# A four-layer fp32 trunk on one core: the two halves of each split weight side by side, and weight buffers at another spacing

## The chip, the core and the metric

The kernel runs on one core of one Trainium2 chip. The metric is the device time of one execution in microseconds (us). The kernel before took 2257.87 us, the median of three runs (2257.78 to 2258.11).

A core has five engines that run side by side and meet only through semaphores: TensorE (in the profile PE, and PEld for its weight loads), VectorE (DVE), ScalarE (ACT), GpSimd (POOL) and SyncE (SP), which here issues the transfers. A matmul on PE holds one operand still in its array (the weights, loaded by an instruction of its own, LDWEIGHTS) and streams the other, the moving operand, past it. Both are read from the on-chip memory SBUF, which has 128 partitions; a "word" below is one fp32 number in each partition.

## What is computed

One sequence of 256 tokens of width 2048 goes through two layers in fp32, each a mixer and a gated feed-forward part, and a last RMSNorm. What matters here is the many products of activations with large weight matrices; attention, scans and norms are small beside them.

```python
h = x
for layer in range(2):
    hn = rms_norm(h, mix_norm_w[layer])
    mix = even_mixer(hn, ...) if layer % 2 == 0 else odd_mixer(hn, od_w_in[0], od_w_out[0])
    h = h + mix
    hn = rms_norm(h, ffn_norm_w[layer])
    g = causal_dwconv(hn @ w_gate[layer], conv_w[layer], conv_b[layer])   # 2048 -> 5632
    h = h + (silu(g) * (hn @ w_up[layer])) @ w_down[layer]                # 5632 -> 2048
return rms_norm(h, final_norm_w)
```

## The kernel before, in words

**Split operands.** Every large product is made from two fp32r parts of each operand: `hi`, the value rounded to fp32r by a copy, and `lo`, what the rounding left over. Three of the four cross products are summed: hi by hi, hi by lo, and lo by hi. An activation tile (`x`, `o` or `act` in the profile) is 128x512: 256 tokens of hi, then 256 tokens of lo.

**A panel.** Weights come from memory in panels of four row blocks (`CH` = 4) of 128 rows and 256 columns, 512 KB each. `prep` (L111) makes one panel ready: SP issues its transfer into a `raw` tile (L122), ACT writes hi with a cast (L127, `hl<-raw`), and DVE writes lo as raw minus hi (L128, `hl<-raw,hl`). Both halves go into one tile `hl`, in the order (c t n): block c, half t (0 is hi, 1 is lo), column n. So 256 words of hi stand ahead of 256 words of lo, and every run that is read or written is 256 words long. The pool `wraw` has four buffers and `whl` three; an `hl` buffer is 4*544 + 8 = 2184 words, so its three buffers start 2184 words apart.

**Three ways to use a panel.** `chan` (L143) takes the weights as the operand that stays in the array: each 128 columns of one half of `hl` are loaded (LDWEIGHTS), and an activation tile streams past. A hi half (L149) meets all 512 words of the activation tile, hi and lo at once; a lo half (L158) meets the 256 hi words alone. A panel has 4 blocks x 2 column halves, so 8 matmuls of 512 and 8 of 256. Their order: six hi matmuls (three blocks of each column half), four lo, one hi, four lo, one hi. `tok` (L161) is the other way round: activations stay, and `hl` streams, for the attention values (L168, L175) and the first panel group (L180). `wide` (L355) does the same with panels of 2 blocks by 512 columns in the last product of the kernel (L361), where the second half of a panel's six matmuls per token tile uses lo.

**Who uses which.** `products` (L184) walks over a stage's jobs and panels: it calls `prep`, then the job's kind, then lets one step of the background work (attention, scan, norms) be emitted by `tick`. The gate and up products of both feed-forward parts, q and k of both mixers, the convolution and gate inputs of the even one, both output projections and the first down projection (`project`, L321) are `chan`; `finish` (L366) calls `prep` itself and uses `wide`.

**What sets the order.** The engines run their instructions in program order. A cast waits for its transfer and for its `hl` buffer to be free, that is for the last matmul of the panel three before it. A hi matmul waits for the cast (ACT), a lo matmul for the subtraction (DVE).

Of the kernel before, what the change touches and what calls it, by code (L numbers as in the profile page):

```python
# [10 lines left out]
F32R = mybir.dt.float32r  # L11
# [4 lines left out]
P = 128  # L16
# [6 lines left out]
CH = 4  # L23
# [38 lines left out]
class Trunk:  # L62
# [45 lines left out]
        return self.params[:, o : o + n]  # L108


    def prep(self, src, pieces=1, between=None):  # L111

        nc = self.nc
        ch, ncol = src.shape[-2:]
        raw = self.wraw.tile([P, CH * 272], F32, tag="raw", name=self.nm("raw"))[:, : ch * ncol]
        hl = self.whl.tile([P, CH * 544 + 8], F32R, tag="hl", name=self.nm("hl"))[:, : 2 * ch * ncol]
        raw = raw.rearrange("p (c n) -> p c n", n=ncol)
        hl = hl.rearrange("p (c t n) -> p c t n", t=2, n=ncol)
        n = ch // pieces
        parts = [slice(i * n, (i + 1) * n) for i in range(pieces)]  # L120
        for i, s in enumerate(parts):
            nc.sync.dma_start(raw[:, s], src[:, s])  # L122
            if between is not None:
                between(i)
        for s in parts:
            hi, lo = hl[:, s, 0, :], hl[:, s, 1, :]
            nc.scalar.copy(hi, raw[:, s])  # L127
            nc.vector.tensor_tensor(lo, raw[:, s], hi.bitcast(F32), ALU.subtract)  # L128
        return hl
# [55 lines left out]
    def products(self, jobs, xs, order=None, late=False):  # L185

        state = [None] * len(jobs)
        waiting = []  # L190

        def chunk(i, ci):
            kind, panel, done = jobs[i]
            od = order or range(panel.shape[0])
            if ci == 0:
                state[i] = self.banks(self.aux if late and i == 2 else self.acc)
            if late and i == ci == 0:
                hl = self.prep(panel[od[ci]], CH, xs.load)
            else:
                hl = self.prep(panel[od[ci]])  # L200
            kind(state[i], hl, xs, od[ci] * CH, ci == 0, ci == len(od) - 1)
            if waiting and i == 2 and ci:
                waiting.pop(0)()
            if ci == len(od) - 1:
                if late and i < 2:
                    waiting.append(lambda: done(state[i]))
                else:
                    done(state[i])
            self.tick()

        n = [j[1].shape[0] for j in jobs]
        for ci in range(n[0]):
            chunk(0, ci)
            chunk(1, ci)
        for i in range(2, len(jobs)):
            for ci in range(n[i]):
                chunk(i, ci)
# [774 lines left out]
```

## Time and profile before

| | |
|---|---|
| time, median of 3 | 2257.87 us |
| profiled execution, its own time | 2258.26 us |
| its span, first to last instruction | 2256.5 us |
| mean granted TensorE clock | 0.999 |
| weights and other data read from memory | 410.86 MB, 183 GB/s over the span |
| transfer of one 512 KB panel, issue to landing | 3.5 us (median) |
| mean busy share of the transfer engines | 55.5% for the queue of the panels |

How to read it: a row of a group names line, engine, operation, out<-in tiles and shapes, then the count; behind the bar stand the busy time in us, the mean of one in ns, and the idle time of the engine just ahead of the group, with what ended it. Matmuls overlap, so the mean of one (some 390 ns for a 512-wide one) is its way through the array and not what it adds; what it adds is the distance from its start to the next start. In the timeline, neighbours of one kind are merged: start, length, engine, line, and how many (x4).

### The profile page before, as it was taken

How to read it: one execution, taken by the hardware profiler on the slowest of the kernel's cores; microseconds unless marked ns; L12 is line 12 of the kernel's file. 1: busy time of each engine (PE TensorE's matmuls, PEld its weight loads, DVE VectorE, ACT ScalarE, POOL GpSimd, SP SyncE). 2: the span in 40 equal slices, each digit the busy share in tenths (PEclk: the TensorE clock that was granted, in tenths of full speed). 3: DMA queues.
4: the chain of work that ended last, by engine and by line, in shares of the span. 5: the costliest groups of instructions: out<-in, count | busy, mean ns of one | idle time of the engine just before them, and what ended most of it. 6: DMA issues, size and time to landing. Idle time of an engine off the chain costs nothing.

```text
span 2256.5 us, 32580 instructions
## 1 busy us (share of the span) xinstructions
PE 2240.3 (99%) x12554; PEld 1941.8 (86%) x12554; DVE 1451.5 (64%) x2025; ACT 1140.9 (51%) x1690; POOL 197.1 (9%) x202
## 2 busy tenths in 40 slices
PE   8999999999999999999999999999999999999998
PEld 7888888888888888888888888888888888888886
DVE  7767767666666665555566656676666666654444
ACT  7555554555555554444444444546555555553343
POOL 3014111101010100000000000110010101000000
PEclk9999999999999999999999999999999999999999
DMA  6654455555555555555555555565555555555554
GB/s 230 189 178 142 152 180 187 186 188 188 190 190 188 187 187 189 189 190 188 187 176 170 172 166 177 177 204 185 180 188 187 189 191 188 187 188 192 189 190 155
DMA packets 116251, 415.08 MB, mean 184 GB/s; under 512 B 12912, under 2 KB 15488, under 8 KB 115968
## 3 DMA queue, kind: packets, MB, share of 16 engines
q1 hardware_dynamic: 115776, 412.48, 55.5%
q8 instruction: 98, 1.61, 0.3%
q14 instruction: 57, 0.47, 0.1%
q10 hardware_dynamic: 288, 0.52, 0.1%
q0 software_dynamic: 32, 0.01, 0.0%
HBM read 410.86 MB, written 2.10 MB: 183 GB/s over the span
## 4 chain that ended last, share of the span: by engine, by line
PE 98%; DVE 0%; ACT 0%; DMA 0%; issue 0%; SPq 0%; POOL 0%; DVEq 0%
PE acc L149 52%; PE acc L158 27%; PE acc L361 11%; PE acc L168 4%; PE acc L175 2%; PE aux L556 0%; PE aux L587 0%; DMA raw<-in_wev 0%; PE acc L180 0%; PE aux L578 0%; PE aux L817 0%; PE aux L539 0%; PE aux L797 0%; PE aux L555 0%; PE aux L588 0%
## 5 line engine op out<-in xcount | busy, mean ns | idle before, releaser
L128 DVE TENSOR_TENSOR hl<-raw,hl 128x1024 fp32r<-128x1024 f32 (+1 forms) x779 | 958.1, 1231 | 712.4 <-ACT hl L127 711.9
L127 ACT CAST hl<-raw 128x1024 fp32r<-128x1024 f32 (+1 forms) x779 | 814.3, 1046 | 872.4 <-PE acc L149 600.4
L149 PE MATMUL acc<-x,hl 128*128 128x512 f32 x3904 | 1078.3, 395 | 0.0
L149 PEld LDWEIGHTS acc<-x,hl 128*128 128x128 f32 x3904 | 700.5, 188 | 106.7 <-issue 0.7
L158 PEld LDWEIGHTS acc<-x,hl 128*128 128x128 f32 x3904 | 596.5, 188 | 64.7
L158 PE MATMUL acc<-x,hl 128*128 128x256 f32 x3904 | 618.3, 280 | 0.0
L361 PE MATMUL acc<-hl,act 128*128 128x512 f32 x1056 | 243.4, 392 | 0.0
L361 PEld LDWEIGHTS acc<-hl,act 128*128 128x128 f32 x1056 | 198.2, 188 | 45.1
L149 PE MATMUL acc<-act,hl 128*128 128x512 f32 x704 | 192.2, 394 | 0.0
L229 ACT COPY ev<-acc 128x256 f32<-128x256 f32 x244 | 90.9, 373 | 162.1 <-PE acc L149 162.1
L457 POOL TENSOR_TENSOR cv<-cv,rbc 128x256 f32<-128x256 f32 x88 | 93.5, 1081 | 880.0 <-ACT cv L456 880.0
L149 PEld LDWEIGHTS acc<-act,hl 128*128 128x128 f32 x704 | 126.3, 188 | 19.4
L149 PE MATMUL acc<-o,hl 128*128 128x512 f32 x512 | 140.9, 395 | 0.0
L299 POOL TENSOR_TENSOR sum<-sum,sq 128x256 f32<-128x256 f32 x67 | 62.3, 929 | 731.9 <-ACT sq L298 723.6
L158 PEld LDWEIGHTS acc<-act,hl 128*128 128x128 f32 x704 | 107.5, 188 | 11.7
L230 DVE TENSOR_TENSOR ev<-acc,ev 128x256 f32<-128x256 f32 x244 | 102.5, 421 | 22.2 <-ACT ev L229 18.3
L158 PE MATMUL acc<-act,hl 128*128 128x256 f32 x704 | 111.4, 280 | 0.0
L149 PEld LDWEIGHTS acc<-o,hl 128*128 128x128 f32 x512 | 92.0, 188 | 14.2
L168 PE MATMUL acc<-hl,x 128*128 128x512 f32 x352 | 103.3, 401 | 0.0
L158 PEld LDWEIGHTS acc<-o,hl 128*128 128x128 f32 x512 | 78.3, 188 | 8.6
L158 PE MATMUL acc<-o,hl 128*128 128x256 f32 x512 | 81.1, 280 | 0.0
L168 PEld LDWEIGHTS acc<-hl,x 128*128 128x128 f32 x352 | 61.1, 188 | 7.9 <-DVE k L618 0.3
(173 smaller groups left out, 1081.0 us busy)
## 6 DMA issues: line engine op xcount, KB each, us to landing
raw<-in_wg SPq DMA_DIRECT2D x176, 512.0 KB, 3.5
raw<-in_wu SPq DMA_DIRECT2D x176, 512.0 KB, 3.5
raw<-in_wd SPq DMA_DIRECT2D x176, 512.0 KB, 3.5
raw<-in_wod SPq DMA_DIRECT2D x96, 512.0 KB, 3.5
raw<-in_wev SPq DMA_DIRECT2D x84, 512.0 KB, 3.5
raw<-in_wevo SPq DMA_DIRECT2D x32, 512.0 KB, 4.0
raw<-in_wodo SPq DMA_DIRECT2D x32, 512.0 KB, 3.5
h<-in_x SPq DMA_DIRECT2D x16, 128.0 KB, 4.8
```

The costliest lines, as they stand in the source:

```text
L127: nc.scalar.copy(hi, raw[:, s])
L128: nc.vector.tensor_tensor(lo, raw[:, s], hi.bitcast(F32), ALU.subtract)
L149: mm(accs[nt], hl[:, k, 0, nt * P : (nt + 1) * P], xs[k0 + k], start=start and k == 0, stop=stop and k == CH - 1,)
L158: mm(accs[nt][:, :T], hl[:, k, 1, nt * P : (nt + 1) * P], xs[k0 + k][:, :T], start=False, stop=False)
L168: both = lambda k: mm(accs[tt], part(xs[k0 + k], 0, tt), hl[:, k].rearrange("p t n -> p (t n)"), start=start and k == 0, stop=stop and k = ...
L175: mm(accs[tt][:, :T], part(xs[k0 + k], 1, tt), hl[:, k, 0, :], start=False, stop=False)
L229: nc.scalar.copy(t, acc[:, T:])
L230: nc.vector.tensor_tensor(t, acc[:, :T], t, ALU.add)
L299: nc.gpsimd.tensor_tensor(sums[-1], sums[-1], sq, ALU.add)
L361: self.nc.tensor.matmul(acc, part(xs[k0 + k], p), hl[:, k, w, :], start=start and n == k == 0, stop=stop and n == 2 and k == ch - 1,)
L457: nc.gpsimd.tensor_tensor(c, c, self.rbc, ALU.mult)
```

## The change

`prep` gets an argument `pairs`. With it, `hl` is laid out in the order (c n t): for each block and column, hi and lo are neighbours. Hi is then every second word from word 0, lo every second from word 1. The cast writes every second word; the subtraction reads hi at every second word and writes lo at every second; a weight load of `chan` reads 128 words out of a stretch of 256. `products` asks for it wherever the job's kind is `chan`, apart from the very first panel, which is a `tok` one. Panels of `tok` and `wide` keep the old order.

Every `hl` tile, of all three kinds, is also made 8 words longer (2192 words) and used from word 16 on, so its buffers start 2192 words apart rather than 2184, and everything placed behind them moves by a little.

```diff
-    def prep(self, src, pieces=1, between=None):
+    def prep(self, src, pieces=1, between=None, pairs=False):
...
-        hl = self.whl.tile([P, CH * 544 + 8], F32R, tag="hl", name=self.nm("hl"))[:, : 2 * ch * ncol]
+        hl = self.whl.tile([P, CH * 544 + 16], F32R, tag="hl", name=self.nm("hl"))[:, 16 : 16 + 2 * ch * ncol]
         raw = raw.rearrange("p (c n) -> p c n", n=ncol)
-        hl = hl.rearrange("p (c t n) -> p c t n", t=2, n=ncol)
+        if pairs:
+            hl = hl.rearrange("p (c n t) -> p c t n", t=2, n=ncol)
+        else:
+            hl = hl.rearrange("p (c t n) -> p c t n", t=2, n=ncol)
...
-                hl = self.prep(panel[od[ci]])
+                hl = self.prep(panel[od[ci]], pairs=kind == self.chan)
```

No instruction is added, taken away or moved on any engine. On DVE and ACT one thing shows in the rows of the program: a panel's split is one run in the new order where it had four. DVE near its start before, in program order (operation, out<-in tiles, shape; the first row is a panel of `chan`, the last but one a panel of `tok`):

```order
L128 TENSOR_TENSOR hl_181<-raw_180,hl_181 128x4x256 [waits DMAHW0_49,Activation_49]
L306 SCALAR_TENSOR_TENSOR x_202<-h_83,first,x_202 128x256 [waits DMAHW1_49,Activation_49]
L306 SCALAR_TENSOR_TENSOR x_206<-h_83,first,x_206 128x256 [waits DMAHW2_49,Activation_49]
L306 SCALAR_TENSOR_TENSOR x_210<-h_83,first,x_210 128x256 [waits DMAHW3_49,Activation_49]
L306 SCALAR_TENSOR_TENSOR x_214<-h_83,first,x_214 128x256 [waits DMAHW4_49,Activation_49]
L128 TENSOR_TENSOR hl_229<-raw_228,hl_229 128x4x272 [waits DMAHW5_49,Activation_49]
L128 TENSOR_TENSOR hl_258<-raw_257,hl_258 128x4x256 [waits DMAHW6_49,Activation_49]
```

The same place of the changed kernel (its lines are numbered 4 higher):

```order
L132 TENSOR_TENSOR hl_181<-raw_180,hl_181 128x1024 [waits DMAHW0_49,Activation_49]
L310 SCALAR_TENSOR_TENSOR x_202<-h_83,first,x_202 128x256 [waits DMAHW1_49,Activation_49]
L310 SCALAR_TENSOR_TENSOR x_206<-h_83,first,x_206 128x256 [waits DMAHW2_49,Activation_49]
L310 SCALAR_TENSOR_TENSOR x_210<-h_83,first,x_210 128x256 [waits DMAHW3_49,Activation_49]
L310 SCALAR_TENSOR_TENSOR x_214<-h_83,first,x_214 128x256 [waits DMAHW4_49,Activation_49]
L132 TENSOR_TENSOR hl_229<-raw_228,hl_229 128x4x272 [waits DMAHW5_49,Activation_49]
L132 TENSOR_TENSOR hl_258<-raw_257,hl_258 128x1024 [waits DMAHW6_49,Activation_49]
```

Only the shape differs, on 640 rows of DVE and on 640 casts of ACT; order and waits are the same.

On PE the one difference is in `wide`, at the kernel's end. The first six matmuls of the first panel there, before (hl_18420 streams; act_14032 and act_14039 are the weights):

```order
L361 MATMUL acc_18417<-hl_18420,act_14032 128x512 [waits Activation_49]
L361 MATMUL acc_18417<-hl_18420,act_14039 128x512 [waits DVE_49]
L361 MATMUL acc_18417<-hl_18420,act_14032 128x512
L361 MATMUL acc_18417<-hl_18420,act_14039 128x512
L361 MATMUL acc_18417<-hl_18420,act_14032 128x512
L361 MATMUL acc_18417<-hl_18420,act_14039 128x512
```

And of the changed kernel:

```order
L365 MATMUL acc_18417<-hl_18420,act_14032 128x512 [waits Activation_49]
L365 MATMUL acc_18417<-hl_18420,act_14039 128x512
L365 MATMUL acc_18417<-hl_18420,act_14032 128x512
L365 MATMUL acc_18417<-hl_18420,act_14039 128x512
L365 MATMUL acc_18417<-hl_18420,act_14032 128x512 [waits DVE_49]
L365 MATMUL acc_18417<-hl_18420,act_14039 128x512
```

The wait for DVE's subtraction stands three matmuls later, at the first one that uses lo; this is so in each of the 88 panels of `wide`.

## The prediction

> **What bounds the kernel now.** The page's busy shares come first, then the clock row, then the chain that ended last with its shares by line.
>
> ```profile
> span 2256.5 us, 32580 instructions
> PE 2240.3 (99%) x12554; PEld 1941.8 (86%) x12554; DVE 1451.5 (64%) x2025; ACT 1140.9 (51%) x1690; POOL 197.1 (9%) x202
> PEclk9999999999999999999999999999999999999999
> by line: PE acc L149 52.4%; PE acc L158 26.6%; PE acc L361 10.8%; PE acc L168 3.6%; PE acc L175 1.8%; PE aux L556 0.3%; PE aux L587 0.3%; DMA raw<-in_wev 0.2%; PE acc L180 0.2%; PE aux L578 0.2%; issue 0.2%; PE aux L817 0.2%; PE aux L539 0.
> ```
>
> PE is busy throughout at full clock, and the chain is PE alone. A busy PE need not be PE at its peak, so I look for waits inside it: the matmul groups of `chan`.
>
> ```profile
> L149 PE MATMUL acc<-x,hl 128*128 128x512 f32 x3904 | 1078.3, 395 | 0.0
> L158 PE MATMUL acc<-x,hl 128*128 128x256 f32 x3904 | 618.3, 280 | 0.0
> L149 PE MATMUL acc<-act,hl 128*128 128x512 f32 x704 | 192.2, 394 | 0.0
> L158 PE MATMUL acc<-act,hl 128*128 128x256 f32 x704 | 111.4, 280 | 0.0
> L149 PE MATMUL acc<-o,hl 128*128 128x512 f32 x512 | 140.9, 395 | 0.0
> L158 PE MATMUL acc<-o,hl 128*128 128x256 f32 x512 | 81.1, 280 | 0.0
> ```
>
> No idle time stands ahead of any of them. There are 3904 + 704 + 512 = 5120 hi matmuls and as many lo ones; 8 of each make a panel, so 640 panels change their order of words. By the chain a hi matmul takes 52.4% of 2256.5 us / 5120 = 230.9 ns, a lo one 26.6% of it / 5120 = 117.2 ns. The kernel is a row of such slots, and only what lengthens or shortens a slot, or starves PE, can move the time. The timeline shows the slots, with the weight loads below them.
>
> ```profile
> 1001.71 1.79 PE L149 MATMUL acc<-act,hl 128*128 128x512 f32 x7
> 1003.33 0.64 PE L158 MATMUL acc<-act,hl 128*128 128x256 f32 x4
> 1003.81 0.39 PE L149 MATMUL acc<-act,hl 128*128 128x512 f32 x1
> 1004.04 0.64 PE L158 MATMUL acc<-act,hl 128*128 128x256 f32 x4
> 1004.52 1.79 PE L149 MATMUL acc<-act,hl 128*128 128x512 f32 x7
> ...
> 1008.95 0.62 PE L158 MATMUL acc<-act,hl 128*128 128x256 f32 x4
> 1009.40 0.39 PE L149 MATMUL acc<-act,hl 128*128 128x512 f32 x1
> ```
>
> ```profile
> 1003.10 0.66 PEld L158 LDWEIGHTS acc<-act,hl 128*128 128x128 f32 x4
> 1003.70 0.19 PEld L149 LDWEIGHTS acc<-act,hl 128*128 128x128 f32 x1
> 1003.82 0.19 PEld L158 LDWEIGHTS acc<-act,hl 128*128 128x128 f32 x1
> ```
>
> A panel lasts 1004.52 - 1001.71 = 2.81 us. A load starts as the matmul before its own starts (1003.82 against 1003.81), so it is hidden by one slot and no more. How long the load occupies its path comes from two widths.
>
> ```profile
> L149 PEld LDWEIGHTS acc<-x,hl 128*128 128x128 f32 x3904 | 700.5, 188 | 106.7 <-issue 0.7 <-ACT ev L229 0.2 <-ACT v L631 0.2
> L817 PEld LDWEIGHTS aux<-ex,ssd 128*64 128x64 f32 x32 | 1.6, 134 | 2.0 <-issue 2.0
> ```
>
> 64 columns more cost 188 - 134 = 54 ns, so 128 columns take some 108 ns of reading. **In a lo slot that leaves 117.2 - 108 = 9 ns; in a hi slot 123 ns.** This margin carries the prediction: a slower load is paid 5120 times in lo slots, and hidden in hi slots until it takes over twice as long.
>
> **The change part by part.** (1) Strided weight loads, 10,240 of them. No row shows a load with a stride, so I bound it. If each word costs what it costs now, 108 ns still fit: nothing. If two words came with one access and now only one is used, the load takes 216 ns: hi slots still hide it (230.9), lo slots grow by 216 - 117.2 = 98.8 ns, times 5120 = +506 us. Between these, the nearest row is the moving operand of the same slot: L158 streams 256 adjacent words in 117.2 ns. A strided load crosses the same 256 words. The moving path thus covers at least that stretch in one lo slot; a load path of like width would need up to 117.2 ns, and with the 9 ns that now follow a load, up to 126 ns: +9 x 5120 = +46 us. I take nothing, since the moving path proves that 256 adjacent words per slot can be delivered, and keep +46 us as an end.
>
> [...]
>
> (2) The cast and the subtraction with a stride.
>
> ```profile
> L128 DVE TENSOR_TENSOR hl<-raw,hl 128x1024 fp32r<-128x1024 f32 x772 | 951.8, 1233 | 707.9 <-ACT hl L127 707.7
> L127 ACT CAST hl<-raw 128x1024 fp32r<-128x1024 f32 x772 | 809.6, 1049 | 871.5 <-PE acc L149 600.4 <-PE acc L361 139.6 <-ACT cv L456 36.9
> ```
>
> ```profile
> 1004.99 1.05 ACT L127 CAST hl<-raw 128x1024 fp32r<-128x1024 f32 x1 [1.76 <-PE acc L149]
> 1006.08 1.23 DVE L128 TENSOR_TENSOR hl<-raw,hl 128x1024 fp32r<-128x1024 f32 x1 [1.52 <-ACT hl L127]
> ```
>
> No row has a stride here either: the ends are nothing and double. The cast starts when PE gives up the buffer (1004.99) and the subtraction ends at 1007.31. The three buffers give the panel to PE two panels later, at about 1004.99 + 2 x 2.81 = 1010.6, so the chain of the two has 3.3 us to spare; doubled (+1.05 + 1.23 = 2.28 us) it still arrives. What can run out is DVE's total. Its load by stage:
>
> ```profile
> 30.00:430.00 400.00, 399.09 (x2319) 345.81 (x2318) 295.13 (x461) 218.57 (x340) 64.18 (x61) 1.00 0.53 173
> 430.00:560.00 130.00, 130.00 (x747) 113.66 (x746) 87.73 (x128) 68.89 (x104) 13.22 (x12) 1.00 0.57 189
> 560.00:1000.00 440.00, 440.00 (x2517) 384.35 (x2516) 278.31 (x380) 220.73 (x314) 35.26 (x33) 1.00 0.57 188
> 1500.00:1650.00 150.00, 150.00 (x873) 131.29 (x872) 101.24 (x157) 82.67 (x127) 13.25 (x18) 1.00 0.57 190
> 1650.00:2000.00 350.00, 350.00 (x2003) 305.72 (x2003) 235.56 (x344) 188.20 (x283) 34.76 (x32) 1.00 0.57 188
> ```
>
> (The third pair is DVE, the fourth ACT.) In the first stage DVE has 400 - 295.13 = 104.9 us free for some 130 such panels (400 / 2.81 = 142, less a dozen of `tok`), 0.8 us each: L128 may go from 1.23 to 2.0 us unseen. Doubled, it overruns by 295 + 160 - 400 = 55 us there; with 46, 157, 53 and 125 panels (length / 2.81) in the other four the overruns are 14, 31, 17 and 39 us: +156 us in all. ACT doubled needs 1140.9 + 640 x 1.05 = 1813 us, under the span. I take no cost: the spare 0.8 us hides a stretch of 60%.
>
> (3) The moved wait of `wide`, and its new start address.
>
> ```profile
> L361 PE MATMUL acc<-hl,act 128*128 128x512 f32 x1056 | 243.4, 392 | 0.0
> ```
>
> No idle time is ahead of L361, so a wait that comes three matmuls later gives nothing back.
>
> (4) Where the words lie. The same slot is not always equally long: four lo slots take 1003.81 - 1003.33 = 0.48 us in one panel and 1009.40 - 1008.95 = 0.45 us in another, 120 and 112.5 ns each, with DVE, ACT and transfers at the same work. What PE reads together may thus meet in SBUF. Until now the load crossed 128 words while the moving operand crossed 256; with the stride both cross 256 in like time, and all buffers start on multiples of 16 words, so the meeting can become constant, for better or worse. If every lo slot were the shortest one: (117.2 - 112.5) x 5120 = 24 us; hi slots in proportion, 230.9 x 4.7 / 117.2 = 9.3 ns x 5120 = 47 us; together **-71 us**. If every one were the longest: 2.8 x 5120 = 14 us, and 28 us in hi slots, +42 us, about the end of part (1). Which way the phase falls no row tells; I take nothing.
>
> **The sum.** Against the profiled execution's own 2258.26 us (span 2256.5 and 1.8 around it; 0.4 us over the median): 0 + 0 + 0 + 0, so 2258 us. About 0.2% (4.5 us) is what a measurement of this kernel can tell from no change.
>
> **The rivals.**
> - *Faster by a better phase.* Slots between their present mean and the shortest seen: 2258 - 71 = 2187 at its end. For it: slots differ with nothing else differing. Against it: a hi slot is 230.9 - 117.2 = 113.7 ns longer than a lo one for 256 more words, and its load of 108 ns fills only its first half, so most of the length follows the moving words, not the load. A part beyond that end is possible. An unsplit fp32 matmul streams 256 words in about 216 ns (next rows: L587's pair to L588, 0.43 us for two), fewer words per ns than here. Were hi slots to reach 216 ns and lo ones 108, it would give 14.9 + 9.2 = 24.1 ns x 5120 = -123 us, 2135 us.
>
> ```profile
> 1161.55 0.59 PE L587 MATMUL aux<-dap,v 128*128 128x256 f32 x2
> 1161.98 0.38 PE L588 MATMUL aux<-dap,v 128*128 128x128 f32 x2
> ```
>
> - *Slower: the load outgrows the lo slot a little.* The mechanism is part (1): from 117 ns on, each ns is 5.1 us. At 126 ns: 2258 + 46 = 2304. For it: a margin of 9 ns, and twice the stretch to read.
> - *Slower by much.* Single words cost the load path double: 2258 + 506 = 2764; or DVE's double: 2258 + 156 = 2414. For it: nothing in the trace, which has no such access; against it, the moving path's width. [...]
>
> **How the numbers follow.** No change within 0.2%: 0.30. Faster within the shortest slots seen: 0.30; beyond: 0.06. Slower by up to 46 us: 0.22. Slower by much: 0.12. The first is the likeliest single time, 2258 us with its own range of 2253.5 to 2262.5: the faster case has the same chance, but spread over some 70 us. The range from 2187 to 2304 leaves out 0.06 + 0.12 = 0.18. Faster 0.36, same 0.30, slower 0.34.
>
> **What would show it.** LDWEIGHTS of L153 and L162 (L149 and L158 now) stay at 188 ns if the stride is free; 296 ns would mean double. The four-slot steps of L162 in the timeline tell 112 from 120 or 126 ns. The mean of L132 (now 1233 ns) against 2.0 us, and L131 (1049), tell of DVE and ACT. Idle time ahead of the matmuls, with DVE as releaser, would mean that the split starves PE. The prediction is wrong if slots change together, in either direction, by over half a percent.

## The result, and the profile after

| | before | after |
|---|---|---|
| time, median | 2257.99 us (4 runs, 2257.78 to 2258.30) | 2276.76 us (4 runs, 2276.32 to 2277.22) |
| ratio to before | 1 | 1.0083, 95% interval 1.0066 to 1.0100 |
| span of the profiled execution | 2256.5 us | 2275.5 us |

The changed kernel is 18.8 us slower, 0.83%. The page of the changed kernel: busy shares, granted clock, and the chain by engine.

```profile
span 2275.5 us, 32580 instructions
PE 2259.4 (99%) x12554; PEld 1991.7 (88%) x12554; DVE 1453.6 (64%) x2025; ACT 1186.0 (52%) x1690; POOL 196.8 (9%) x202
PEclk9999999999999999999999999999999999999999
PE 98%; DVE 1%; ACT 1%; issue 0%; DMA 0%; SPq 0%; POOL 0%; DVEq 0%
```

The kind of limit is the same: PE busy throughout (99%), at full clock (0.999 granted), and the chain is PE (98%). VectorE's total has hardly moved (1453.6 us, 1451.5 before), ScalarE's has grown by 45 us beside the chain. What grew is PE's own work, and the weight loads. The groups of the changed kernel, loads first, then casts and subtractions, then matmuls (lines are 4 higher than before: L153 hi, L162 lo, L365 the last product):

```profile
L153 PEld LDWEIGHTS acc<-x,hl 128*128 128x128 f32 x3904 | 727.4, 196 | 90.6 <-issue 0.5 <-ACT v L635 0.2 <-ACT ev L233 0.2
L162 PEld LDWEIGHTS acc<-x,hl 128*128 128x128 f32 x3904 | 614.1, 196 | 54.8
L365 PEld LDWEIGHTS acc<-hl,act 128*128 128x128 f32 x1056 | 198.3, 188 | 48.1
...
L132 DVE TENSOR_TENSOR hl<-raw,hl 128x1024 fp32r<-128x1024 f32 x772 | 951.7, 1233 | 733.1 <-ACT hl L131 728.0
L131 ACT CAST hl<-raw 128x1024 fp32r<-128x1024 f32 x772 | 859.7, 1114 | 854.1 <-PE acc L153 550.3 <-PE acc L365 142.6 <-ACT cv L460 34.9
...
L153 PE MATMUL acc<-x,hl 128*128 128x512 f32 x3904 | 1082.0, 396 | 0.0
L162 PE MATMUL acc<-x,hl 128*128 128x256 f32 x3904 | 625.4, 282 | 0.0
L365 PE MATMUL acc<-hl,act 128*128 128x512 f32 x1056 | 246.6, 395 | 0.0
```

A strided load takes 196 ns by its record where it took 188; the loads of L365, whose weights are activations without a stride, stay at 188. The cast takes 1114 ns (1049 before), the subtraction 1233 as before. No matmul group has idle time ahead of it, so nothing starves PE: its slots are longer. The last product grew as well (246.6 us against 243.4), though its panels keep the old order of words. The timeline of PE in the changed kernel, over one panel, shows the slots:

```profile
1001.32 0.65 PE L162 MATMUL acc<-act,hl 128*128 128x256 f32 x4
1001.81 1.80 PE L153 MATMUL acc<-act,hl 128*128 128x512 f32 x7
1003.45 0.65 PE L162 MATMUL acc<-act,hl 128*128 128x256 f32 x4
1003.93 0.40 PE L153 MATMUL acc<-act,hl 128*128 128x512 f32 x1
1004.17 0.64 PE L162 MATMUL acc<-act,hl 128*128 128x256 f32 x4
1004.64 1.81 PE L153 MATMUL acc<-act,hl 128*128 128x512 f32 x7
```

A panel takes 1004.64 - 1001.81 = 2.83 us (2.81 before). The steps are printed in hundredths, too coarse for differences of 2 ns. So for every run below, the distances from each matmul's start to the next start were summed over the whole trace, by kind: "lo" and "hi" are the 5120 matmuls each of `chan`, "last" the product at the kernel's end. These sums are what the experiments are read by, beside the load's recorded length.

| us | lo | hi | last | load, ns |
|---|---|---|---|---|
| before | 602.2 | 1194.7 | 243.0 | 188 |
| after | 612.0 | 1201.1 | 246.2 | 196 |
| difference | +9.8 | +6.4 | +3.2 | +8 |

The three differences make 19.4 us; the spans differ by 19.0.

### The profile page after: what moved, and what is told of

Same layout as the page of the kernel before. It is cut to its first block, busy times and chain, and to the rows that moved or that the text cites. A ratio compares the mean times of both kernels' runs of the same rounds, so it can differ in the third digit from the quotient of the medians.

```text
span 2275.5 us, 32580 instructions
## 1 busy us (share of the span) xinstructions
PE 2259.4 (99%) x12554; PEld 1991.7 (88%) x12554; DVE 1453.6 (64%) x2025; ACT 1186.0 (52%) x1690; POOL 196.8 (9%) x202
## 4 chain that ended last, share of the span: by engine, by line
PE 98%; DVE 1%; ACT 1%; issue 0%; DMA 0%; SPq 0%; POOL 0%; DVEq 0%
PE acc L153 52%; PE acc L162 27%; PE acc L365 11%; PE acc L172 3%; PE acc L179 2%; PE aux L560 0%; PE aux L591 0%; DMA raw<-in_wev 0%; ACT hl L131 0%; PE acc L184 0%; PE aux L582 0%; DVE hl L132 0%; PE aux L821 0%; PE aux L543 0%; PE aux L592 0%
## 5 line engine op out<-in xcount | busy, mean ns | idle before, releaser
L131 ACT CAST hl<-raw 128x1024 fp32r<-128x1024 f32 (+1 forms) x779 | 864.5, 1110 | 854.7 <-PE acc L153 550.3
L153 PE MATMUL acc<-x,hl 128*128 128x512 f32 x3904 | 1082.0, 396 | 0.0
L153 PEld LDWEIGHTS acc<-x,hl 128*128 128x128 f32 x3904 | 727.4, 196 | 90.6 <-issue 0.5
L162 PEld LDWEIGHTS acc<-x,hl 128*128 128x128 f32 x3904 | 614.1, 196 | 54.8
L162 PE MATMUL acc<-x,hl 128*128 128x256 f32 x3904 | 625.4, 282 | 0.0
L365 PE MATMUL acc<-hl,act 128*128 128x512 f32 x1056 | 246.6, 395 | 0.0
L365 PEld LDWEIGHTS acc<-hl,act 128*128 128x128 f32 x1056 | 198.3, 188 | 48.1
L153 PE MATMUL acc<-act,hl 128*128 128x512 f32 x704 | 193.8, 397 | 0.0
L153 PEld LDWEIGHTS acc<-act,hl 128*128 128x128 f32 x704 | 131.8, 197 | 16.5
L153 PE MATMUL acc<-o,hl 128*128 128x512 f32 x512 | 141.1, 395 | 0.0
L162 PEld LDWEIGHTS acc<-act,hl 128*128 128x128 f32 x704 | 111.3, 196 | 10.1
L162 PE MATMUL acc<-act,hl 128*128 128x256 f32 x704 | 113.3, 284 | 0.0
L153 PEld LDWEIGHTS acc<-o,hl 128*128 128x128 f32 x512 | 95.3, 195 | 11.9
L162 PEld LDWEIGHTS acc<-o,hl 128*128 128x128 f32 x512 | 80.5, 196 | 7.4
L162 PE MATMUL acc<-o,hl 128*128 128x256 f32 x512 | 81.9, 282 | 0.0
```

The source lines that it names most:

```text
L153: mm(accs[nt], hl[:, k, 0, nt * P : (nt + 1) * P], xs[k0 + k], start=start and k == 0, stop=stop and k == CH - 1,)
L162: mm(accs[nt][:, :T], hl[:, k, 1, nt * P : (nt + 1) * P], xs[k0 + k][:, :T], start=False, stop=False)
L365: self.nc.tensor.matmul(acc, part(xs[k0 + k], p), hl[:, k, w, :], start=start and n == k == 0, stop=stop and n == 2 and k == ch - 1,)
```

## The experiments

Three theories stood at the start. **S**: the stride lengthens each load, and lo slots pay. **P**: the new places of the buffers do it. **W**: the strided writes of ScalarE and VectorE disturb what PE reads. The first four kernels each make one part of the change alone.

**The new order alone.** The changed kernel with the old tile:

```diff
-        hl = self.whl.tile([P, CH * 544 + 16], ...)[:, 16 : 16 + 2 * ch * ncol]
+        hl = self.whl.tile([P, CH * 544 + 8], ...)[:, : 2 * ch * ncol]
```

> The new order of words alone, with buffers at the old spacing (2184 words, from word 0). Theory S (the stride makes each weight load longer, 188 to 196 ns, and lo slots pay for it): loads at 196 ns, lo and hi slots of the 640 panels some 15.6 us longer in all, the last product (L361 of before) back at 230.4 ns a matmul, time 2273 to 2275 us. Rival P (the new places of the buffers do it, the stride nothing): loads at 196 ns or not, but time within 4 us of before, 2254 to 2262. Rival W (the strided writes of ScalarE and VectorE disturb PE): 2273 to 2275 too; the next two runs tell S from W.

Measured: 2272.34 us, ratio 1.0062 (1.0049 to 1.0074), where S and W had 2273 to 2275. The order of words carries 14.2 us of the 18.8. P alone falls, and the last product is back at its old length (243.5 us busy).

**The new spacing alone.** The kernel before with the new tile:

```diff
-        hl = self.whl.tile([P, CH * 544 + 8], ...)[:, : 2 * ch * ncol]
+        hl = self.whl.tile([P, CH * 544 + 16], ...)[:, 16 : 16 + 2 * ch * ncol]
```

> The new spacing alone (2192 words, from word 16), the old order of words. S: loads at 188 ns, the slots of the 640 panels as before, only the last product longer by 3 ns a matmul (3.2 us): 2261 us. P: all of the loss, 2274 to 2279 us. W: as S.

Measured: 2257.07 us, ratio 0.9996 (0.9987 to 1.0004): no change. Its groups are not unchanged, though. The last product in this run:

```profile
L361 PE MATMUL acc<-hl,act 128*128 128x512 f32 x1056 | 246.6, 395 | 0.0
```

The last product is 3.2 us longer, as S expected; the `chan` slots got 3.7 us shorter (lo 600.4, hi 1192.8), which no theory had expected, and the two cancel. So the 2261 us of S was missed as well.

**Strided loads of panels written as before.** Each load takes every second word of the old layout:

```diff
+        flat = hl.rearrange("p c t n -> p c (t n)")
+        def pick(k, t, nt):
+            o = 2 * nt * P + t
+            return flat[:, k, o : o + 255 : 2]
...
-                    accs[nt], hl[:, k, 0, nt * P : (nt + 1) * P], xs[k0 + k],
+                    accs[nt], pick(k, 0, nt), xs[k0 + k],
```

> Panels are written in the old order at the old spacing, but each weight load of chan takes every second word of a stretch of 256 (so it takes other words than it should: the output is not the reference's). S: loads at 196 ns, time 2273 to 2275 us, the cast back at 1049 ns. W: 2258 us, since the writes run without a stride. P: 2258 us.

Measured: 2271.89 us, ratio 1.0060 (1.0048 to 1.0073). The groups of this run:

```profile
L127 ACT CAST hl<-raw 128x1024 fp32r<-128x1024 f32 x772 | 809.2, 1048 | 883.9 <-PE acc L154 609.4 <-PE acc L366 139.6 <-ACT cv L461 38.2
L154 PEld LDWEIGHTS acc<-x,hl 128*128 128x128 f32 x3904 | 725.2, 195 | 90.8 <-issue 0.5 <-ACT hl L127 0.2 <-ACT ev L234 0.2
L163 PEld LDWEIGHTS acc<-x,hl 128*128 128x128 f32 x3904 | 615.3, 196 | 55.9
```

The casts write as before and take 1048 ns; the loads are at 195 to 196 ns and the loss is all there (lo 612.2, hi 1198.4, last 243.1). Some hi matmuls now read words of the lo half and so depend on the subtraction, but PE waited for a subtraction only once, for 0.6 us, in a `tok` panel. S holds in this: the strided loads make the loss, with no strided write near them.

**Strided writes, loads without a stride.** Panels in the new order, each load takes 128 adjacent words:

```diff
+        flat = hl.rearrange("p c t n -> p c (n t)")
+        def pick(k, t, nt):
+            o = t * 2 * P + nt * P
+            return flat[:, k, o : o + 128 : 1]
```

> Panels are written in the new order (cast and subtraction with a stride) at the old spacing, but each weight load takes 128 adjacent words (a mix of hi and lo, so the output is not the reference's). S: loads at 188 ns, time 2258 us within 4 us, the cast at 1114 ns. W: 2273 to 2275 us with loads at 188 ns.

Measured: 2258.94 us, ratio 1.0003 (0.9994 to 1.0012): no change. The groups of this run:

```profile
L131 ACT CAST hl<-raw 128x1024 fp32r<-128x1024 f32 x772 | 856.7, 1110 | 839.6 <-PE acc L158 542.7 <-PE acc L370 139.6 <-ACT act L320 34.0
L158 PEld LDWEIGHTS acc<-x,hl 128*128 128x128 f32 x3904 | 701.1, 188 | 107.2 <-DVE q L621 0.3 <-issue 0.3 <-DVE k L627 0.2
```

The cast is slow, the load is not, and the time is that of before. W falls.

**What a load pays for.** The next three stretch the stride in the same way as the strided loads above, to every third, fourth and eighth word. They tell whether the price is that of lines touched, of a threshold in the step, or of the stretch crossed. A line here is a group of four adjacent words (16 bytes). That a load pays by such lines was the author's assumption, and these runs test it. The diff is the one for a step of three.

```diff
-            o = 2 * nt * P + t
-            return flat[:, k, o : o + 255 : 2]
+            o = 2 * nt + t
+            return flat[:, k, o : o + 382 : 3]
```

> Old order, old spacing; each weight load of chan takes every third word (128 words out of a stretch of 382; other words than it should, so the output is not the reference's). Theory S with lines (a load pays for each 16-byte line it touches: 64 lines took 116 ns, so 1.81 ns a line): 96 lines, 174 ns, recorded loads of 254 ns, lo slots of 178 ns, about +307 us: 2565 us. Rival L (any step under four words costs the same): loads at 196 ns, 2272 us.

> As before it, with every fourth word (128 words out of 509; the output is not the reference's). S with lines: 128 lines, 232 ns, recorded loads of 312 ns, lo slots of 236 ns, hi slots 3 to 4 ns longer, about +620 us: 2880 us. Rival L: the load takes double of 108 ns from a step of four words on: recorded loads of 296 ns, +524 us, 2782 us.

> As before it, with every eighth word (128 words out of 1017; the output is not the reference's). S with lines: still one line a word, 128 lines, so the same as a step of four: loads of 312 ns, 2880 us. Rival: the load pays for the stretch that it crosses, so double of a step of four: loads over 500 ns, over 5000 us.

Measured in one execution each: 2574.16, 2877.65 and 2961.15 us, beside 2257.88 for the kernel before. The loads, a step of three first, then four, then eight:

```profile
L154 PEld LDWEIGHTS acc<-x,hl 128*128 128x128 f32 x3904 | 919.1, 257 | 1.4 <-issue 0.7 <-DVE sbl L521 0.2 <-DVE q L617 0.2
L163 PEld LDWEIGHTS acc<-x,hl 128*128 128x128 f32 x3904 | 826.0, 260 | 0.0
```

```profile
L154 PEld LDWEIGHTS acc<-x,hl 128*128 128x128 f32 x3904 | 1016.9, 318 | 1.4 <-issue 0.9 <-DVE sbl L521 0.2
L163 PEld LDWEIGHTS acc<-x,hl 128*128 128x128 f32 x3904 | 999.5, 323 | 0.0
```

```profile
L154 PEld LDWEIGHTS acc<-x,hl 128*128 128x128 f32 x3904 | 1051.8, 332 | 1.2 <-issue 0.9 <-DVE sbl L521 0.2
L163 PEld LDWEIGHTS acc<-x,hl 128*128 128x128 f32 x3904 | 1034.8, 334 | 0.0
```

By the prediction's two widths, some 188 - 108 = 80 ns of a recorded length are not reading; that is an estimate, from one row of 32 loads. Less that part, with the lengths of the lo loads (L163):

| step, words | lines of four words that a load touches | load, ns | ns a line | lo + hi, us | added per lo matmul |
|---|---|---|---|---|---|
| 1 | 32 | 108 | 3.4 | 1796.9 | |
| 2 | 64 | 116 | 1.81 | 1810.6 | 2.7 ns |
| 3 | 96 | 180 | 1.88 | 2114.9 | 62 ns |
| 4 | 128 | 243 | 1.90 | 2418.3 | 121 ns |
| 8 | 128 | 254 | 1.98 | 2501.6 | 138 ns |

(Added: the difference to 1796.9, over 5120.) The threshold falls, since a step of three, under four words, already costs 62 ns. The stretch falls, since it doubles from four to eight words while the load grows by 11 ns. That the load grows with the step up to four words (116, 180, 243 ns) and hardly beyond (254 ns) is what lines of four words give. A price of 1.8 to 2.0 ns for each line touched carries steps two to eight: it gave 2565 and 2880 us for three and four, against 2574 and 2878 measured. For a step of eight it gave 2880 too, 81 us under the measured time, so something small beyond the count of lines is left. At a step of one it does not hold: 32 lines at 1.81 ns would be 58 ns. The 108 ns there come from the two widths, 54 / 64 = 0.84 ns a column, and no run shows what sets them.

Where a load's excess is booked is seen in the timeline too. PE with a step of four words, then the loads:

```profile
1302.37 0.98 PE L163 MATMUL acc<-act,hl 128*128 128x256 f32 x4
1303.19 0.51 PE L154 MATMUL acc<-act,hl 128*128 128x512 f32 x1
1303.54 0.98 PE L163 MATMUL acc<-act,hl 128*128 128x256 f32 x4
```

```profile
1302.14 1.01 PEld L163 LDWEIGHTS acc<-act,hl 128*128 128x128 f32 x4
1303.05 0.33 PEld L154 LDWEIGHTS acc<-act,hl 128*128 128x128 f32 x1
```

The four lo slots take 0.82 us and the hi slot behind them 0.35 us, where that one took 0.23 us before: of four excesses one is booked on the hi slot. The first of the four lo loads starts at 1302.14, before the lo slots do, and is hidden; the load of the next hi matmul starts at 1303.05, under the last lo slot. So four loads run under four lo slots, one of them a hi matmul's, and some of the hi column above is paid for loads that ran under lo slots.

**Where the buffers lie.** The spacing did nothing alone, but 2276.76 - 2272.34 = 4.4 us on top of the stride. The intervals of the two ratios overlap, so this rests on the traces: the last product is 3.1 us longer, as it is without the stride, and the `chan` slots are 1.9 us longer, where without the stride they got 3.7 us shorter. Two kernels in the old order vary start and distance apart from each other. The diff is the first one's; in the second every panel but those of 272 columns starts at word 16, in the old tile of 2184 words.

```diff
+        at = 16 if kind == self.chan else 0
+        hl = self.whl.tile([P, CH * 544 + 16], ...)[:, at : at + 2 * ch * ncol]
```

> Old order of words. Buffers 2192 words apart; chan panels start at word 16, tok and wide panels at word 0. If the start of the streamed panel makes the last product longer: its matmuls back at 230.4 ns, chan slots as with the new spacing alone, 2254 us. If the distance between the buffers does it: 233.4 ns, 2257 us.

> Old order of words. Buffers 2184 words apart as before, but panels (apart from the three of 272 columns) start at word 16. If the start makes the last product longer: 233.4 ns there, and chan slots 0.4 ns shorter, 2257 us. If the distance does it: 230.4 ns and chan slots as before, 2258 us.

Measured: 2256.05 us (0.9992, 0.9983 to 1.0001) and 2266.68 us (1.0039, 1.0026 to 1.0051). The first came out as distance had it, the second as neither. So neither the start nor the distance decides alone: the last product took 246.0 and 244.6 us, the hi slots 1192.0 and 1198.6, the lo slots 600.5 and 604.8. Both theories fall. The first of the two is the fastest kernel measured, but its interval takes in no change.

The last three set the distance to multiples of 64 words: 2176, 2240 and 2304.

> Old order of words, buffers start at word 0 and stand 2176 words apart (8 fewer than before; a multiple of 64 words). So far hi and lo slots and the last product moved with the place of the buffers by up to 1.5% each, with no rule found. If what counts is the distance between what a load and a stream read, modulo 64 words: this, the next and the one behind it behave alike, within 2 us of each other. If the absolute place counts, they differ from each other by 2 to 10 us. Between 2250 and 2268 us.

> As before it, 2240 words apart (35 x 64). Modulo 64 words: within 2 us of the run before it. Absolute place: differs. Between 2250 and 2268 us.

> As before it, 2304 words apart (9 x 256, so each buffer starts at the same place modulo 256 words). Modulo 64 words: within 2 us of the two before it. Modulo 256: the panels of all three buffers last equally long, which they did not at 2184. Between 2250 and 2268 us.

Measured: 2258.38, 2258.44 and 2258.46 us, ratio 1.0002 each (0.9993 to 1.0012 for the first two, 0.9993 to 1.0011 for the third). Nearly the same to the last digit inside: lo 608.8, 608.9, 608.9; hi 1185.5, 1186.3, 1186.1; last 246.2 in all three. And within each run the panels of the three buffers (every third panel in the order of `prep`; medians) last equally long, 2793 to 2794 ns, where at 2184 words they last 2787, 2797 and 2810. That what counts is the place modulo 64 words, or modulo 32, fits these runs. Modulo 16 does not: with the new spacing alone the buffers agree with these modulo 16, and the sums differ (lo 600.4, hi 1192.8). Their split differs from before (lo 6.6 us more, hi 9.2 less, last 3.2 more); the sum does not.

## Why the prediction was right or wrong

The measured 2276.76 us lies in the range (2187 to 2304), but not where the likeliest case had it (2258): the small slowdown with a chance of 0.22 came. That it lies in the range says little, since the range spans both directions and the chances were near even (faster 0.36, same 0.30, slower 0.34). By the prediction's own sign, slots that change together by over half a percent, it was wrong: lo slots grew by 1.6%, hi slots by 0.5%, the last product by 1.3%.

- **What bounds the kernel**: right. The time moved as the slots did, and no engine beside PE mattered.
- **Part (1), strided loads: the step that failed.** Who pays, the lo slots, and the ends of 0 and 9 ns were right; the value taken was not. "I take nothing, since the moving path proves that 256 adjacent words per slot can be delivered" drew the wrong conclusion from the right row. Order alone cost 14.2 us (lo 612.3, hi 1198.9 against 602.2 and 1194.7), 2.8 ns a lo matmul. The term should have been taken between the ends rather than at the lower one.
- **"From 117 ns on, each ns is 5.1 us"**: not borne out as it stands. A load of 116 ns would have been free by this rule, and it was not. But the 116 rests on the 80 ns that are not reading, and the steps of three, four and eight words give other values: loads under hi slots, which nothing holds up, are recorded there at some 252, 310 and 328 ns, and lo slots that wait for a load last 176, 234 and 242 ns, which is 76, 76 and 86 ns less. The load of the changed kernel, some 195 ns under hi slots, so reads for 109 to 119 ns. Whether it outgrows the slot by a little, or load and stream hold each other up within it as part (4) supposes, no run here tells.
- **"Hi slots hide it"**: right of the load, which stayed below a hi slot in the changed kernel (196 ns by its record, against 1201.1 us / 5120 = 234.6 ns). The hi slots grew all the same, since the load of a hi matmul behind lo ones runs under a lo slot: with the order alone the two hi slots of a panel that stand behind lo ones grew by 5.1 and 1.1 ns, the other six by 0.3 ns together.
- **Part (2), cast and subtraction**: right. The cast grew by 6% (1049 to 1114 ns), the subtraction by nothing (1233 ns in both), and with strided writes alone the time was that of before.
- **Part (3), the moved wait**: right that it gives nothing back. But the heading named the new start address as well and the working gave it no price: with the new spacing the last product takes 3.2 us more in either order.
- **Part (4), where the words lie**: right that places matter and that the sign could not be told; the spacing had an effect of its own, +4.4 us on top of the stride, between -2 and +9 us over the other spacings tried in the old order. The rival of a better phase came in no kernel: the lowest, 2256.05 us, is far from 2187.
- **Slower by much**: did not happen, and the steps of three and four words show how near it was. One more word of stride, tried on panels in the old order, was +316 us.

## What to carry to other kernels

Where one engine bounds a kernel, write its time as a sum of slots and find in each what hides under what, and with how many ns to spare; a slowdown of a hidden instruction is then a number times a count. A margin of 9 ns in 117 is no margin when the hidden instruction is to read out of twice the stretch (here its record grew from 188 to 196 ns, and the kernel by 14.2 us): where the ends are 0 and 9 ns and nothing tells between them, do not take the lower end. When two edits come together, run each alone: here the stride cost 14.2 us alone, the spacing nothing alone, and the spacing 4.4 us on top of the stride.

## What the runs showed that was not expected

**Near-equal paces on three engines.** ScalarE's cast wrote 1024 words with a stride in 1114 ns and without in 1049; VectorE's subtraction took 1233 ns either way. Two widths of each, from the profile of before (the wide ones stand in the prediction), give their pace:

```profile
L312 DVE TENSOR_TENSOR act<-ev,act 128x256 fp32r<-128x256 f32 x88 | 33.2, 420 | 0.0
L311 ACT CAST act<-ev 128x256 fp32r<-128x256 f32 x88 | 32.7, 407 | 1.0 <-DVE ev L466 1.0
```

The paces that follow are estimates from these rows. The cast needs (1049 - 407) / 768 = 0.84 ns a word, 1.67 ns for two; the subtraction (1233 - 420) / 768 = 1.06 ns, 2.12 ns for two. With a stride the cast slowed by 65 / 512 = 0.13 ns for two words, to 1.80, and the subtraction, slower than that already, not at all. The strided load took 116 / 64 = 1.81 ns for two words. And the moving operand of a hi slot, 512 adjacent words in 230.9 ns by the chain (233.3 from start to start), takes 1.80 to 1.82 ns for four words. Whether these like figures have one cause was not shown; no run tests it.

**The place modulo 64 words.** Three distances that agree modulo 64 words gave the same kernel within 0.1 us of time and 1 us of every sum; others moved hi slots, lo slots and the last product by up to 1.5% each, mostly against one another. Whether accesses meet there, and why the places favour one kind of slot at the other's cost, stays open.
